# More streamed products in two inverses, an input split behind a mask step, and other PSUM banks for second spans

## The chip, the cores and the metric

The kernel runs on one core of one Trainium2 chip. The metric is the device time of one launch in microseconds. Three launches of the kernel before gave 970.76, 971.34 and 972.85 us; the median is 971.34. Engines are named as in the profile: PE is the matmul engine (TensorE), DVE VectorE, ACT ScalarE, POOL GpSimd, and SP (SyncE) issues most DMAs.

## The reference

One layer of a hybrid decoder on 512 prompt tokens and 8 sequences of 8 new tokens, 576 columns in all. Two branches read the same normalised input: an RWKV-7 branch ("a", 8 heads of 64, a recurrent state per head) and a differential attention ("b"). Their outputs are merged by gates, and a squared-ReLU MLP and a final norm follow.

```python
xn = rmsnorm(x, g_mix)
P = xn @ w_in                                   # 1024 -> RWKV, q/k/v and gate columns
o_a, S = rwkv7_branch(shift_mix(P[:, :1792]), S0)
att = diff_attend(q, k, v, lam)                 # softmax(q1 k1) - lam * softmax(q2 k2)
o_b = rmsnorm(att, subln_g) * (1 - lam_init)
m = gate_a * (o_a @ w_br_a) + gate_b * (o_b @ w_br_b)
x = x + m @ w_out
x = x + square(relu(rmsnorm(x, g_ffn) @ w_up)) @ w_down
y = rmsnorm(x, g_final)
```

In `rwkv7_branch` every step of the state is `S = S * w + (S a) b^T + v k^T`, `y = S r`. The kernel computes it in chunks of 64 tokens.

## The kernel before

**Layout and products.** Channels lie on the 128 partitions, the 576 tokens on the free axis. A float32 product is made from halves: each operand is split into a high half (a copy by ACT in the fp32r type) and a low half (DVE subtracts the high half from the original), and three matmuls are added up in PSUM: high by high, high by low, low by high. The token axis is cut into two spans of 288 columns (`HALF`), so one output block of 128 channels takes 2 spans x the number of 128-row pieces of the contraction x 3 matmuls: 48 for a contraction of 1024, 24 for one of 512. In the profile such a block's weights are `raw_x`, `hi_x`, `lo_x` and its PSUM tile `ps_x`.

**`stream` (L154)** makes such a block as a generator: it loads the weights with SP, splits them, takes one PSUM bank for each span, and yields before each matmul, so that its caller decides between which other instructions the products fall. When a span is finished, an evacuation `evac` reads the bank. `dense` runs a stream to its end at once. `waiting` is a list of streams; `take(n)` puts out the next n products of it, and `fill(n)` does so behind the last matmul issued.

**PSUM.** There are eight banks: two in the pool `psd`, for streams; three in `psw` (`bank`), for short steps; one called `tbank`; and two called `cbank(0)` and `cbank(1)`. The last two hold the scores in attention, and later the steps of the chain.

**The order of the work.** The framework's scheduler sets each engine's instruction order ahead of time by the priority (by default the order in the program), its own estimate of when each instruction could run, and by hand-written constraints: `tc.issue_after(ins)` puts the instructions of a block behind `ins` on the engine of `ins`. On the chip each engine then runs its list in that order.

**The RWKV part.** `rwkv(hp)` (L753) handles a group of two heads, `hp` = 0 to 3, as a generator with stages:

- Stage 1 (to L849) makes decays and keys, and extracts the matrices A of the chunks: matmuls into the banks `pA`, which DVE clips with a mask into `ABR` and `ST` (L843, L847).
- Stage 2 (to L889) makes transposes (`pV`, `pK`) and applies the entering states (`pI`).
- Stage 3 (to L948) inverts the triangular A in four levels. Each level has two visits to PE by `blocks` (L903): 32x32 matmuls into `pW`, copied by ACT into `W`; 32x32 matmuls into `pZ`, which DVE adds to `X` and transposes into `Y`. Behind each visit's small matmuls stand nine streamed products, `take(9)`. Then `pWc` and `pC` follow.
- Stages 4 to 7 finish the samples' states (`pF`), the norm of the output `y` (mean, variance, a power by POOL), and the branch output `oa`, by the transposes `pTy` and the gate product `pg`.

`chain(pr)` (L1016) runs the eight chunks in order for two groups at once, with `cbank` 0 and 1 in turn (`pch`).

The driver (L1106 to L1130) puts the gate columns' streams (`gate`, `ps_g`) on the list, and runs the stages of the four groups with `take` calls between them. The third inverse (hp = 2) and the last one (hp = 3) use up the first five of one half of the gate streams. Then eight streams `branch_b(d)` (`ps_brb`) and the three gate streams left are put on the list, in turn, and `chain(1)` and the last stages follow.

**The second branch.** The attention output lies in DRAM as `ob_d`. `branch_b` calls `ob_halves` (L461) once: four loads into tiles `ob`, four copies by ACT to the high halves and four subtractions by DVE to the low halves (`obh`). Each `branch_b(d)` then loads the gate tile `gb`, streams 24 products, and multiplies the gate tile by each finished span. The tiles `ob` and `gb` share one tag of six buffers.

**After the branches.** At L1143 eight blocks of the first branch's product (`ps_bra`) are evacuated into the merged halves `mh` and `ml`; then come the output projection (`ps_wo`, with a tile `xr` of the input added), the MLP's first layer (`up_pair`, PSUM tiles `ua`, `ub`, `uc`, `ud`, `ux`) and its second (`ps_dn`). The last quarter of the second layer (L1361) runs over the tokens in two unequal spans (320 and 256 columns) with eight streams of one span each; its evacuation writes `fin`.

## Time and profile before

The profile is of one execution.

| | |
|---|---|
| Times of three launches (us) | 970.76, 971.34, 972.85 |
| The profiled execution's own time (us) | 971.81 |
| Its span, first to last instruction (us) | 970.0 |
| Mean granted TensorE clock | 0.996 |
| PE busy | 947.0 us, 10120 matmuls |
| ACT busy | 508.4 us, 1120 instructions |
| DMA | 105.75 MB, mean 109 GB/s |
| The third inverse's visits | from 375.5 us of the span |
| The last inverse's visits | from 402.8 us |
| Chain of the last two groups | 421 to 467 us |
| First branch's product (`ps_bra`) | from 493.8 us |
| MLP's first layer | from 571 us |
| Last quarter of its second layer | 906 to 960 us |

Rows of the profile read like this. A row of a timeline has the start in us from the span's start, the duration in us, engine, line, operation, tiles (out<-in), shapes, the count of merged instructions, and in brackets the idle time of the engine just before, with what ended it. A row of the chain of waits has start, duration and what the end of the kernel depended on. A row of the list of waits has who waited for whom, the total in us, the number of times, and the longest. A line number can be that of a helper: L58 is every ACT copy, L61 every DVE tensor-tensor operation, L72 every matmul. Matmuls are pipelined, and their ends are modelled.

### The profile page before, as it was taken

What the parts mean: (1) busy time and instruction counts of PE and PEld (TensorE: products, weight loads), DVE (VectorE), ACT (ScalarE), POOL (GpSimd) and SP (SyncE); (2) the same over time, 40 slices, a digit from 0 to 9 for tenths busy, and PEclk for the clock granted to TensorE, in tenths of its full rate; (3) what the DMA queues carried; (4) which work ended last, traced back from release to release, by engine and by line L of the source; (5) the groups of instructions that cost most, each with busy time, mean ns of one, the idle gap of its engine ahead of it and who ended that gap; (6) DMA issues with size and microseconds to landing.
All of it is one profiled execution on the core that took longest, in us unless ns stands there. A gap on an engine that the chain in (4) does not pass through costs nothing.

```text
span 970.0 us, 24610 instructions
## 1 busy us (share of the span) xinstructions
PE 947.0 (98%) x10120; PEld 898.3 (93%) x10120; DVE 675.1 (70%) x1435; ACT 508.4 (52%) x1120; POOL 64.6 (7%) x173
## 2 busy tenths in 40 slices
PE   9999999999999998999999999999999999999996
PEld 9999999888987897888999999999999999999996
DVE  6598676776555967455787989866666666666744
ACT  6577465556344564553444767444444444444732
POOL 2601100100000210000100000000000000000001
PEclk9999999999999999999999999999999999999998
DMA  8322663211213234222687532222222222220402
GB/s 271 120 87 91 187 224 117 93 35 47 68 58 102 83 103 168 72 84 74 198 260 236 159 95 98 92 88 88 87 88 88 88 87 88 87 88 23 142 1 97
DMA packets 50833, 105.75 MB, mean 109 GB/s; under 512 B 6066, under 2 KB 8114, under 8 KB 50594
## 3 DMA queue, kind: packets, MB, share of 16 engines
q1 hardware_dynamic: 47442, 96.95, 30.8%
q0 software_dynamic: 1648, 5.35, 1.6%
q10 hardware_dynamic: 1632, 1.89, 0.6%
q8 instruction: 79, 1.29, 0.6%
q14 instruction: 32, 0.26, 0.1%
HBM read 89.38 MB, written 14.78 MB: 107 GB/s over the span
## 4 chain that ended last, share of the span: by engine, by line
PE 56%; DVE 2%; ACT 1%; issue 1%; DMA 1%; POOL 0%; DVEq 0%
PE ps_dn L72 21%; PE ua L1275 5%; PE ux L1275 5%; PE ps_wo L72 4%; PE ps_g L72 4%; PE ps_bra L72 3%; PE uc L1275 3%; PE ub L1275 3%; PE ps_brb L72 3%; PE ud L1275 2%; PE pch L1032 2%; DMA raw_dn<-in_w_down_dram 1%; PE pZ L72 1%; PE pW L72 1%; DVE ya L61 0%
## 5 line engine op out<-in xcount | busy, mean ns | idle before, releaser
L72 PE MATMUL ps_dn<-q,hi_dn 128*128 128x288 f32 x768 | 154.7, 296 | 0.0
L72 PEld LDWEIGHTS ps_dn<-q,hi_dn 128*128 128x128 f32 x768 | 122.8, 188 | 1.4
L72 PE MATMUL ps_dn<-q,lo_dn 128*128 128x288 f32 x384 | 113.2, 295 | 0.0
L72 PE MATMUL ps_g<-xh,lo_g 128*128 128x288 f32 x256 | 78.8, 308 | 0.0
L72 PE MATMUL ps_g<-xl,hi_g 128*128 128x288 f32 x256 | 77.7, 304 | 0.0
L72 PE MATMUL ps_g<-xh,hi_g 128*128 128x288 f32 x256 | 77.4, 302 | 0.0
L72 PEld LDWEIGHTS ps_dn<-q,lo_dn 128*128 128x128 f32 x384 | 72.0, 188 | 0.0
L72 PE MATMUL ps_z<-xh,lo_z 128*128 128x288 f32 (+1 forms) x224 | 69.7, 311 | 0.0
L72 PE MATMUL ps_z<-xl,hi_z 128*128 128x288 f32 (+1 forms) x224 | 67.1, 299 | 0.0
L72 PE MATMUL ps_z<-xh,hi_z 128*128 128x288 f32 (+1 forms) x224 | 66.9, 299 | 0.0
L61 DVE TENSOR_TENSOR ya<-ya,ps_dn 128x288 f32<-128x288 f32 x96 | 43.3, 451 | 27.6 <-PE ps_dn L72 27.5
L58 ACT ACTIVATE hi_dn<-raw_dn 128x512 fp32r<-128x512 f32 x48 | 30.1, 628 | 56.2 <-PE ps_dn L72 56.1
L58 ACT ACTIVATE c<-c 128x288 f32<-128x288 f32 x112 | 48.7, 440 | 9.4 <-DVE c L61 7.7
L1275 PE MATMUL ux<-h_t,hi 128*128 128x288 f32 x256 | 52.4, 296 | 0.0
L1275 PE MATMUL ua<-h_b,hi 128*128 128x288 f32 x256 | 52.2, 296 | 0.0
L58 ACT ACTIVATE hi<-a 128x1024 fp32r<-128x1024 f32 (+1 forms) x32 | 27.1, 846 | 43.2 <-PE ps_dn L72 34.9
L72 PEld LDWEIGHTS ps_g<-xh,lo_g 128*128 128x128 f32 x256 | 48.1, 188 | 1.5 <-issue 0.2
L72 PEld LDWEIGHTS ps_g<-xh,hi_g 128*128 128x128 f32 x256 | 48.2, 188 | 1.3 <-issue 0.2
L72 PEld LDWEIGHTS ps_g<-xl,hi_g 128*128 128x128 f32 x256 | 48.2, 188 | 1.3 <-issue 0.2
L72 PE MATMUL ps_dn<-q,w 128*128 128x320 f32 (+1 forms) x336 | 46.6, 298 | 0.4 <-DVE fin L61 0.4
L61 DVE TENSOR_TENSOR lo<-s,hi 128x1024 fp32r<-128x1024 f32 x32 | 39.2, 1224 | 10.2 <-ACT hi L58 10.0
L72 PEld LDWEIGHTS ps_dn<-q,w 128*128 128x128 f32 x336 | 45.2, 190 | 0.8 <-DVE fin L61 0.7
(390 smaller groups left out, 2721.4 us busy)
## 6 DMA issues: line engine op xcount, KB each, us to landing
a<-in_w_up_dram SPq DMA_DIRECT2D x32, 512.0 KB, 3.3
raw_dn<-in_w_down_dram SPq DMA_DIRECT2D x64, 256.0 KB, 2.7
raw_g<-in_w_in_dram SPq DMA_DIRECT2D x32, 256.0 KB, 3.0
raw_z<-in_w_in_dram SPq DMA_DIRECT2D x28, 256.0 KB, 2.9
gt_d<-gg SPq DMA_DIRECT2D x16, 288.0 KB, 2.4
g<-gt_d SPq DMA_DIRECT2D x16, 288.0 KB, 4.0
kp<-in_ktab_dram SPq DMA_DIRECT2D x16, 256.0 KB, 3.7
vp<-in_vtab_dram SPq DMA_DIRECT2D x16, 256.0 KB, 3.6
```

Source lines behind the costliest of these rows:

```text
L58: ring["act"] = AE.activation(out=out, in_=in_, func=func, **kw)
L61: ins = (eng or VE).tensor_tensor(out=out, in0=a, in1=b, op=op)
L72: ring["mm"] = PE.matmul(out=out, lhsT=lhsT, rhs=rhs, start=start, stop=stop)
L1032: ring["mm"] = PE.matmul(out=ps[rows, e], lhsT=lhs, rhs=rhs, start=first and e == 1, stop=True, skip_group_check=True)
L1275: ring["mm"] = PE.matmul(out=ps[:, :288], lhsT=l[:, k], rhs=hb[blk][:, h, k], start=start and i == 0, stop=i == 11, skip_group_check=skip)
```

## The change

There are three parts.

1. `blocks` puts ten streamed products behind each visit in place of nine when `hp` is 2 or 3.
2. The four high and four low halves of the second branch's input (`ob_halves`) are ordered behind stage 1 of the last group. At its end, stage 1 keeps the last ACT instruction and the last DVE tensor-tensor instruction issued (`own["cut"]`); the latter is the last clip of A, the former the copy of `ST` ahead of the extraction. The high halves go behind the one, the low halves behind the other.
3. `stream` gets an argument `pick`, a list with a `cbank` number or `None` for each span. The second span of `branch_b(d)` for d >= 3 and of every `ps_bra` block goes to `cbank(d % 2)`. In the last quarter of the second MLP layer the streams with odd d go to `cbank(d // 2 % 2)`.

```diff
     def stream(src, kt, xh, xl, spans, evac, name, raws=None, together=False, banks=None,
-               keep=None):
+               keep=None, pick=None):
...
-        pss = banks or [psd.tile([P, 512], F32, tag="d", name=f"ps_{name}_{i}") for i in range(len(spans))]
+        pss = banks or [cbank(pick[i], f"ps_{name}_{i}") if pick and pick[i] is not None else
+                        psd.tile([P, 512], F32, tag="d", name=f"ps_{name}_{i}") for i in range(len(spans))]
...
-            act(hi[h][:, :NT], o_)
-            tt(lo[h][:, :NT], o_, f32(hi[h][:, :NT]), SUB)
+            with tc.issue_after(pair[1]["cut"][0].ins):
+                act(hi[h][:, :NT], o_)
+            with tc.issue_after(pair[1]["cut"][1].ins):
+                tt(lo[h][:, :NT], o_, f32(hi[h][:, :NT]), SUB)
         return hi, lo
 
+    pair = {}
     ob = []
...
-        yield from stream(w_brb[d], HB, ob[0], ob[1], HALF, ev, f"brb_{d}")
+        yield from stream(w_brb[d], HB, ob[0], ob[1], HALF, ev, f"brb_{d}",
+                          pick=(None, d % 2) if d >= 3 else None)
...
-    pair = {}
     halves = [(par, slice(64 * par, 64 * par + 64)) for par in range(2)]
...
                     tt(clip(ST[par], c0, cn)[oth], x[1][oth], m3(c[oth, mk:mk + P], cn), MUL)
+        own["cut"] = ring["act"], ring["tt"]
...
             with tc.issue_after(last.ins):
-                take(9)
+                take(9 if hp < 2 else 10)
...
-        dense(w_bra[d], HB, [o[:, 0] for o in oab], [o[:, 1] for o in oab], HALF, ev, f"bra_{d}")
+        dense(w_bra[d], HB, [o[:, 0] for o in oab], [o[:, 1] for o in oab], HALF, ev, f"bra_{d}",
+              pick=(None, d % 2))
...
-            s_ = stream(None if t0 else w_down[3, d], KT, qh, ql, ((t0, n),), ev, f"dn3{d}_{t0}", keep=rows[d])
+            s_ = stream(None if t0 else w_down[3, d], KT, qh, ql, ((t0, n),), ev, f"dn3{d}_{t0}", keep=rows[d],
+                        pick=(d // 2 % 2,) if d % 2 else None)
```

## The prediction, made before the changed kernel was run

> **What bounds the kernel now.** I read the page's head first, then the list of TensorE's waits.

> ```profile
> span 970.0 us, 24610 instructions
> PE 947.0 (98%) x10120; PEld 898.3 (93%) x10120; DVE 675.1 (70%) x1435; ACT 508.4 (52%) x1120; POOL 64.6 (7%) x173
> PE pA L72 <- DVE ABR L61: 2.6, 4, 1.5
> PE pZ L72 <- issue: 1.8, 2, 1.1
> PE ps_brb L72 <- DVE gb L66: 1.2, 2, 0.7
> ```

> TensorE is busy for 98% of the span, so no engine can be relieved to much effect; only its 23 us of idle time can be won, and the change removes no matmul. The waits (total us, times, longest) name three candidates near the edits; a fourth, ps_dn after fin, is in the timeline below. An idle figure understates a stop, because a product's modelled end lies 0.29 us after its start while the next one could start much sooner. The pace comes from the chain of waits, and the stops from TensorE's timeline:

> ```profile
> 494.00 25.65 PE ps_bra L72 x192
> 914.13 24.26 PE ps_dn L72 x168
> 371.20 0.40 PE L72 MATMUL ps_g<-xl,hi_g 128*128 128x288 f32 x1
> 373.12 1.29 PE L72 MATMUL pA<-ST,KB 64*64 64x128 f32 x32 [1.52 <-DVE ABR L61]
> 477.14 0.50 PE L72 MATMUL ps_brb<-obh,hi_brb 128*128 128x288 f32 x2 [0.69 <-DVE gb L66]
> 477.48 0.29 PE L72 MATMUL ps_brb<-obh,lo_brb 128*128 128x288 f32 x1
> 492.15 0.53 PE L72 MATMUL ps_brb<-obh,hi_brb 128*128 128x288 f32 x2 [0.55 <-DVE gb L66]
> 912.96 0.75 PE L72 MATMUL ps_dn<-q,w 128*128 128x320 f32 x4
> 914.13 0.70 PE L72 MATMUL ps_dn<-q,w 128*128 128x320 f32 x3 [0.42 <-DVE fin L61]
> ```

> 25.65/192 is 0.134 us a product of 288 columns, 24.26/168 is 0.144 for the last stage's. So a stop loses its idle time plus 0.29 - 0.13 = 0.16, and a little for restarting: after the stop at 477.14 two products take 0.50, so the second starts 0.21 after the first, 0.08 late. At 492.15 that is 0.10, at 914.13 about 0.10.

> **Part 1, the input split behind A.** VectorE and ScalarE around the first stop:

> ```profile
> 369.26 0.45 DVE L61 TENSOR_TENSOR gg<-ps_g,R 128x288 f32<-128x288 f32 x1
> 371.70 0.76 DVE L61 TENSOR_TENSOR obh<-ob,obh 128x576 fp32r<-128x576 f32 x1 [1.99 <-ACT obh L58]
> 372.38 0.88 DVE L61 TENSOR_TENSOR ABR<-pA,cst_sb 128x512 f32<-128x512 f32 x2
> 370.98 0.68 ACT L58 ACTIVATE obh<-ob 128x576 fp32r<-128x576 f32 x1 [1.11 <-DMA ob<-ob_d]
> 369.94 1.32 PE L72 MATMUL pA<-ST,KB 64*64 64x128 f32 x40
> 368.68 4.12 SPq L485 DMA_DIRECT2D gb<-gt_d  x4
> 379.12 0.33 SPq L150 DMA_DIRECT2D raw_g<-in_w_in_dram  x1
> 389.39 0.63 ACT L58 ACTIVATE hi_g<-raw_g 128x512 fp32r<-128x512 f32 x1 [1.40 <-PE ps_g L72]
> ```

> VectorE runs in order. From 369.71 it stood before the low half of the split (obh), which waited for ScalarE's high half, which waited for ob's load. The first group of pA was done at 369.94 + 1.32 = 371.26, but its reader, the ABR clip, stood behind and began at 372.38. TensorE needs the clips to free banks, and lost 373.12 - 371.20 - 0.13 = 1.79. With the low halves behind the last clip the first one can start at about 371.3, **1.1 earlier**; the other 0.7 stays, since TensorE resumes 0.74 after the clips begin. Bounds: 0.4, if another piece of some 0.7 takes the place in front, and all of 1.79, if the order fills it with products. I take 1.1, the row nearest.

> What moves: two low halves (the one at 371.70 and one just before gg; the other two are behind the clips already) come behind them, 2 x 0.76 us; on ScalarE one high half of 0.68 is held until the copy of ST ahead of pA, of no weight. In the SyncE queue the four gb loads (the row of 4.12 us) wait for tiles that the split frees; the last of them will stand until the second low half is done, about 378, with raw_g behind it. That weight load leaves at 379.12 anyway and is first read about 389.39, so even a few us of delay cost 0. Nothing moves on GpSimd's queue.

> Where the two low halves land is the second group's inverse, in front of something that TensorE waits for:

> ```profile
> L61 DVE TENSOR_TENSOR X<-X,pZ 128x288 f32<-128x288 f32 (+1 forms) x4 | 1.7, 436 | 3.8 <-PE pZ L72 3.8
> 388.40 0.42 DVE L61 TENSOR_TENSOR X<-X,pZ 128x256 f32<-128x256 f32 x1 [0.89 <-PE pZ L72]
> 388.36 1.38 PE ps_g L72 x9
> 389.74 0.68 PE pW L72 x50
> 382.76 1.13 issue
> 415.03 1.26 PE ps_g L72 x8
> 416.21 0.75 PE L72 MATMUL pW<-X,DM 32*32 32x32 f32 x64
> 416.90 0.65 PE L76 MATMUL pTy<-cst_sb,y 128*128 128x128 f32 x4
> 417.58 0.95 PE L72 MATMUL pZ<-W,Y 32*32 32x32 f32 x64
> 417.59 2.02 ACT L58 ACTIVATE oa<-pTy 64x256 f32<-64x256 f32 x6
> ```

> Between 375.9 and 395.4 VectorE waits 3.8 us for pZ alone, so 1.5 us fits. X of one visit ends at 388.82, and the pW that reads it starts near 389.7: 0.85 spare. One low half (0.76) in front is just covered.

> **Part 2, ten products a visit.** In these two inverses nine products already cover each visit: 9 take 1.38 with the change of shape, and the next burst follows. So the tenth removes no steady wait; it lengthens the cover by 0.13, to about 0.98, which is what the displaced low halves need. I put gain and cost there at 0 (bounds: 1.5 lost, if both low halves fall where nothing is spare; 0.2 gained at the first pZ).

> The tenth is taken from somewhere. The list of streamed products in front of the second branch runs out in the last inverse: counted in the timeline, its eight visits get 9, 9, 9, 9, 9, 8, 0, 0 = 53. The third inverse will take 8 more, leaving 45 = 10, 10, 10, 10, 5, 0, 0, 0. So the sixth visit is bare too and the fifth half bare: 8 products, 1.07 us, of cover are gone there. The visit at 416.21 shows what a bare one does: four pTy transposes fill it and pZ starts at 417.58. More such work is due there, and the second branch's products have their operands. I charge **0.4** (bounds 0 and 1.07).

> **Part 3, banks for second spans.** Now a product stream's two spans take both `psd` banks, and the next stream waits for an evacuation that stands in VectorE's queue behind other work:

> ```profile
> 475.27 0.76 DVE L61 TENSOR_TENSOR y<-y,var 128x576 f32<-128x576 f32 x1 [1.50 <-POOL var L243]
> 476.56 0.44 DVE L66 SCALAR_TENSOR_TENSOR gb<-gb,ps_brb 128x288 f32<-128x288 f32 x1
> 913.59 0.48 DVE L61 TENSOR_TENSOR fin<-ps_dn,ya 128x320 f32<-128x320 f32 x1
> ```

> With second spans in the chain's banks, idle once the chain has ended, a stream needs only one `psd` bank and the next has the other. Both brb stops go: 0.69 + 0.16 + 0.08 + 0.55 + 0.16 + 0.10 = 1.74. In the last projection the third stream no longer needs the bank of the first: 0.42 + 0.16 + 0.10 = **0.68** (0.3 if the queue that held `fin` holds the next bank as well). The bra stream has no stop in its 25.65 us, so its banks are worth 0 by themselves; they matter for what is late next:

> ```profile
> 493.84:519.49 25.65, 25.65 (x194) 25.65 (x193) 22.93 (x54) 10.72 (x23) 0.00 (x0) 1.00 0.80 252
> 493.65 0.45 DVE L61 TENSOR_TENSOR oab<-oa,oab 128x288 fp32r<-128x288 f32 x1
> 520.80 0.69 DVE L61 TENSOR_TENSOR lo_wo<-raw_wo,hi_wo 128x512 fp32r<-128x512 f32 x1
> 521.89 0.90 SPq L1182 DMA_DIRECT2D xr<-in_xT_dram  x2
> 525.78 0.46 DVE L61 TENSOR_TENSOR ya<-ps_wo,xr 128x288 f32<-128x288 f32 x1 [3.92 <-PE ps_wo L72]
> ```

> In the window of bra (stretch, length, then PE, PEld, DVE busy) VectorE works 22.93 of 25.65 us. The last oab half is first read 21 products into bra, 2.8 us after its start: it ends at 494.1 and is wanted at 496.8, so 2.7 us spare for an earlier arrival of at most 1.74. At the other end the load of xr follows lo_wo, and the evacuation at 525.78 follows the load; if VectorE is late there, TensorE stops for it. About 0.9 of the 1.74 pulls VectorE's own work along (the pTy transposes of the last two groups follow in order behind the first stop); the other 0.8 must come out of its 2.7 us of idle time in bra. I take **1.45** of 1.74 (bounds 0.9 and 1.74).

> **The sum.** 1.1 + 1.45 + 0.68 - 0.4 = 2.83 us. The profiled execution took 971.81 (span 970.0, 1.8 around it), so it would take 968.98. It lies 0.47 above the median of the runs shown, 971.34; from that median the forecast is **968.5**.

> **Instruction supply.** The wait of 1.13 "issue" at 382.76 lies inside one burst of little matmuls (pZ), with no engine to blame, and the second of the two, 0.7, lies in the last inverse. [...]

> **Rivals.**
> 1. *Instruction stops move.* Ten products shift every burst against whatever makes the two stops, now 1.8 together. Against: two stops in sixteen visits are few. If there are two more like these, 2.83 - 1.8 = 1.03 gained: 970.3. (None at all would give 966.7.)
> 2. *VectorE or xr takes over behind brb.* Then 0.2 of the 1.74 remains: 1.1 + 0.2 + 0.68 - 0.4 = 1.58: 969.8. For it: 520.80 to 525.78 is already tight. Against: 2.7 us of idle time in bra.
> 3. *The split does not leave the way.* If ScalarE's high halves, held only behind the copy of ST, or other VectorE work still stand before the clips, the 1.1 is missing: 1.73 gained, 969.6. For it: pA of the other groups waits too, (2.6 - 1.5) over three places.
> 4. *The last inverse runs bare (slower).* If nothing fills visits five to eight, each of 3.5 visits idles some 0.7 (1.37 from the pW at 416.21 to its pZ, less 0.68 of burst), 2.45; with the six oa copies (2.02) in front of one W and the two low halves (1.5) in front of X it is 6.0, against 1.1 + 1.45 + 0.68 = 3.23 won: 2.8 slower, 974.1. It decides once TensorE idles over 3.2 us there. Against: pTy, pg and brb products are ready to fill.

> **Chances.** Forecast 0.60, rival 1 0.10, rival 2 0.13, rival 3 0.09, rival 4 0.08. The range leaves out rival 4 and the far ends. A difference of 0.2% (1.94 us) is about what a measurement of this kernel can tell from no change. Rivals 1 to 3 gain less than that: faster 0.60, same 0.32, slower 0.08. The range takes in rivals 1 to 3 and the upper bounds, 4.2 for the three parts and part of the 1.8 of instruction stops: 966.2 to 971.0.

> **What would show it.** Right: pA's longest wait falls from 1.5 to some 0.5; the waits of ps_brb for gb and of ps_dn for fin vanish from TensorE's list; bra still runs at 0.134 a product; the stop of ps_wo for ya stays under 0.5. Wrong: new waits of pZ, pW or pWc for W or X in the last inverse, "issue" well off 1.8, or ps_wo's wait grown by what brb won.

## The result, and the profile after

Fourteen runs of the changed kernel have a median of 969.34 us (968.59 to 970.70), beside 972.54 us (970.76 to 975.04) for fourteen of the kernel before: ratio 0.9964, 95% interval 0.9956 to 0.9972, so 0.36% faster. The profiled execution took 968.82 us with a span of 967.0, against 971.81 and 970.0.

The head of the page after and TensorE's list of waits (who waited for whom: total us, times, longest):

```profile
span 967.0 us, 24611 instructions
PE 944.7 (98%) x10120; PEld 896.4 (93%) x10120; DVE 675.4 (70%) x1435; ACT 509.2 (53%) x1120; POOL 64.1 (7%) x173
PE pZ L72 <- issue: 1.4, 3, 0.7
PE pA L72 <- DVE ABR L61: 1.3, 4, 0.7
PE ps_wo L72 <- DVE ya L61: 0.7, 1, 0.7
PE pI L72 <- ACT SVU L58: 0.7, 1, 0.7
```

Of the waits that the prediction read, ps_brb for gb and ps_dn for fin are gone, pA's total is halved, ps_wo's for ya has grown, and pI's for SVU is new. The place of the split in the timeline after:

```profile
371.31 0.40 PE L72 MATMUL ps_g<-xl,hi_g 128*128 128x288 f32 x1
371.94 1.29 PE L72 MATMUL pA<-ST,KB 64*64 64x128 f32 x32 [0.24 <-DVE ABR L61]
371.20 0.89 DVE L61 TENSOR_TENSOR ABR<-pA,cst_sb 128x512 f32<-128x512 f32 x2 [1.51 <-PE pA L72]
381.37 1.39 DVE L61 TENSOR_TENSOR obh<-ob,obh 128x576 fp32r<-128x576 f32 x2
377.96 0.33 SPq L150 DMA_DIRECT2D raw_g<-in_w_in_dram  x1
```

The clips begin at 371.20, as soon as pA is done, and no longer at 372.38. From the last gate product to the next pA it is now 0.63 us where it was 1.92: 1.29 won. The four profiles without the split (the kernel before and three of the experiments below) show 1.42, 1.66, 1.92 and 2.05 there, so the gain is 0.8 to 1.4, and 1.1 on average. The low halves stand in the third inverse (two of them at 381.37), and raw_g still leaves at 378, held by the gb loads as forecast.

The two stretches of part 3, each from the first product that could gain to the first instruction behind it: start and end, length, then busy time and count of PE, PEld, DVE, ACT and POOL, the granted clock, DMA share and GB/s. The kernel before:

```profile
473.12:493.84 20.72, 19.48 (x141) 18.46 (x139) 15.59 (x34) 9.98 (x24) 3.60 (x2) 1.00 0.69 221
906.51:959.81 53.30, 52.88 (x395) 52.28 (x394) 30.55 (x66) 22.98 (x49) 2.76 (x3) 1.00 0.21 70
```

The changed kernel:

```profile
472.20:491.19 18.99, 18.99 (x141) 18.42 (x140) 14.69 (x32) 10.00 (x24) 3.60 (x2) 1.00 0.65 214
904.25:956.87 52.62, 52.62 (x396) 52.28 (x395) 30.44 (x66) 22.91 (x48) 2.75 (x3) 1.00 0.22 71
```

The same matmuls, 1.73 and 0.68 us shorter, and in both TensorE is now busy from end to end. What part 3 won in the first stretch is partly lost where the output projection starts. Rows of the changed kernel around its first evacuation:

```profile
518.70 0.69 DVE L61 TENSOR_TENSOR lo_wo<-raw_wo,hi_wo 128x512 fp32r<-128x512 f32 x1
519.79 0.90 SPq L1188 DMA_DIRECT2D xr<-in_xT_dram  x2
523.50 0.46 DVE L61 TENSOR_TENSOR ya<-ps_wo,xr 128x288 f32<-128x288 f32 x1 [3.74 <-DMA xr<-in_xT_dram]
524.01 0.40 PE L72 MATMUL ps_wo<-mh,hi_wo 128*128 128x288 f32 x1 [0.69 <-DVE ya L61]
```

And the same stop in the kernel before:

```profile
526.29 0.40 PE L72 MATMUL ps_wo<-mh,hi_wo 128*128 128x288 f32 x1 [0.26 <-DVE ya L61]
```

The load of xr stands in the SyncE queue behind a load of raw_wo, and that one waits until VectorE's subtraction lo_wo has freed a weight buffer. So xr leaves 1.1 us after lo_wo begins, in both kernels; it lands at 523.4, and TensorE stops 0.69 us for the evacuation, where it stopped 0.26 before. In the kernels with bra's new banks lo_wo begins the later, the longer VectorE has waited in bra for the loads of the gate tiles g. The kernel before and four with these banks, three of them from the experiments below (us; lo_wo and xr are counted from the start of ps_wo):

| Kernel | VectorE waits for g in bra | lo_wo begins | xr leaves | ps_wo waits for ya |
|---|---|---|---|---|
| before | 0.60 | 1.31 | 2.40 | 0.26 |
| all but the split | 1.74 | 1.57 | 2.66 | 0.58 |
| changed | 2.10 | 1.92 | 3.01 | 0.69 |
| banks alone | 3.05 | 2.87 | 3.96 | 1.61 |
| all but the ten products | 3.33 | 3.04 | 4.13 | 1.94 |

The rows go together; no run moved the loads of g, and why they land later in some kernels than in others stays open.

How far TensorE is ahead of the kernel before, by the starts of the same matmuls (us from the span's start):

| Start of | before | after | ahead | change |
|---|---|---|---|---|
| third inverse (first pW) | 375.45 | 374.28 | 1.17 | +1.28, split; -0.11 ahead of it |
| the last matmuls of the chain | 466.14 | 465.22 | 0.92 | -0.25, ten products |
| ps_bra | 493.84 | 491.19 | 2.65 | +1.73, brb's banks |
| ps_wo | 519.49 | 516.78 | 2.71 | +0.06 |
| MLP's first layer (uc) | 571.41 | 569.13 | 2.28 | -0.43, ya |
| last quarter of the second layer | 906.51 | 904.25 | 2.26 | -0.02 |
| last sums (pst) | 959.81 | 956.87 | 2.94 | +0.68, dn's banks |
| end of the span | 970.04 | 967.05 | 2.99 | +0.05 |

The -0.11 is what two chances leave. From 11 us on the changed kernel was 0.55 ahead, after a start that differs between the two profiles, and it lost that in the first two inverses, where stops with no engine to blame take 1.7 us in it and 0.5 in the kernel before.

### The profile page after: what moved, and what is told of

It is laid out like the page before. It is cut to its first block, busy times and chain, and to the rows that moved or that the text cites. A ratio compares the mean times of both kernels' runs of the same rounds, so it can differ in the third digit from the quotient of the medians.

```text
span 967.0 us, 24611 instructions
## 1 busy us (share of the span) xinstructions
PE 944.7 (98%) x10120; PEld 896.4 (93%) x10120; DVE 675.4 (70%) x1435; ACT 509.2 (53%) x1120; POOL 64.1 (7%) x173
## 3 DMA queue, kind: packets, MB, share of 16 engines
q8 instruction: 79, 1.29, 0.6%
## 4 chain that ended last, share of the span: by engine, by line
PE 69%; ACT 3%; DVE 2%; issue 1%; DMA 0%; POOL 0%; DVEq 0%; ACTq 0%
PE ps_dn L72 21%; PE ps_g L72 10%; PE ux L1281 5%; PE ua L1281 5%; PE ps_wo L72 4%; PE pch L1037 3%; PE ps_z L72 3%; PE ud L1281 3%; PE ub L1281 3%; PE ps_bra L72 3%; PE ps_brb L72 3%; PE uc L1281 3%; PE pZ L72 1%; PE pW L72 1%; ACT TT L58 0%
## 5 line engine op out<-in xcount | busy, mean ns | idle before, releaser
L72 PE MATMUL ps_dn<-q,hi_dn 128*128 128x288 f32 x768 | 154.7, 296 | 0.0
L72 PEld LDWEIGHTS ps_dn<-q,hi_dn 128*128 128x128 f32 x768 | 122.8, 188 | 1.4
L72 PE MATMUL ps_dn<-q,lo_dn 128*128 128x288 f32 x384 | 113.2, 295 | 0.0
L72 PE MATMUL ps_g<-xh,lo_g 128*128 128x288 f32 x256 | 78.2, 305 | 0.0
L72 PE MATMUL ps_g<-xh,hi_g 128*128 128x288 f32 x256 | 77.9, 304 | 0.0
L72 PE MATMUL ps_g<-xl,hi_g 128*128 128x288 f32 x256 | 77.9, 304 | 0.0
L72 PEld LDWEIGHTS ps_dn<-q,lo_dn 128*128 128x128 f32 x384 | 72.0, 188 | 0.0
L72 PE MATMUL ps_z<-xh,lo_z 128*128 128x288 f32 (+1 forms) x224 | 69.7, 311 | 0.0
L72 PE MATMUL ps_z<-xl,hi_z 128*128 128x288 f32 (+1 forms) x224 | 67.1, 300 | 0.0
L72 PE MATMUL ps_z<-xh,hi_z 128*128 128x288 f32 (+1 forms) x224 | 66.9, 299 | 0.0
L61 DVE TENSOR_TENSOR ya<-ya,ps_dn 128x288 f32<-128x288 f32 x96 | 43.3, 451 | 27.6 <-PE ps_dn L72 27.5
L58 ACT ACTIVATE hi_dn<-raw_dn 128x512 fp32r<-128x512 f32 x48 | 30.1, 627 | 56.2 <-PE ps_dn L72 56.1
L58 ACT ACTIVATE c<-c 128x288 f32<-128x288 f32 x112 | 48.7, 439 | 9.3 <-DVE c L61 7.6
L58 ACT ACTIVATE hi<-a 128x1024 fp32r<-128x1024 f32 (+1 forms) x32 | 27.1, 846 | 43.3 <-PE ps_dn L72 34.9
L72 PEld LDWEIGHTS ps_g<-xl,hi_g 128*128 128x128 f32 x256 | 48.2, 188 | 1.5 <-issue 0.2
L72 PEld LDWEIGHTS ps_g<-xh,hi_g 128*128 128x128 f32 x256 | 48.2, 188 | 1.4 <-issue 0.2
L72 PEld LDWEIGHTS ps_g<-xh,lo_g 128*128 128x128 f32 x256 | 48.2, 188 | 1.3 <-issue 0.2
L72 PE MATMUL ps_dn<-q,w 128*128 128x320 f32 (+1 forms) x336 | 46.3, 297 | 0.0
L61 DVE TENSOR_TENSOR lo<-s,hi 128x1024 fp32r<-128x1024 f32 x32 | 39.2, 1224 | 10.2 <-ACT hi L58 10.0
L72 PEld LDWEIGHTS ps_dn<-q,w 128*128 128x128 f32 x336 | 45.3, 190 | 0.1
```

Of the source, the lines that this page charges most:

```text
L58: ring["act"] = AE.activation(out=out, in_=in_, func=func, **kw)
L61: ins = (eng or VE).tensor_tensor(out=out, in0=a, in1=b, op=op)
L72: ring["mm"] = PE.matmul(out=out, lhsT=lhsT, rhs=rhs, start=start, stop=stop)
```

## The experiments

Each run was timed in five rounds beside the kernel before (972.3 to 973.1 us there); ratios are to that.

**One part, or all but one.** Six runs: the split alone, the banks alone, ten products alone, all but the ten products, all but the split, all but the banks. The edits put the lines of the kernel before back:

```diff
-                take(9 if hp < 2 else 10)
+                take(9)
...
-            with tc.issue_after(pair[1]["cut"][0].ins):
-                act(hi[h][:, :NT], o_)
-            with tc.issue_after(pair[1]["cut"][1].ins):
-                tt(lo[h][:, :NT], o_, f32(hi[h][:, :NT]), SUB)
+            act(hi[h][:, :NT], o_)
+            tt(lo[h][:, :NT], o_, f32(hi[h][:, :NT]), SUB)
...
-        yield from stream(w_brb[d], HB, ob[0], ob[1], HALF, ev, f"brb_{d}",
-                          pick=(None, d % 2) if d >= 3 else None)
+        yield from stream(w_brb[d], HB, ob[0], ob[1], HALF, ev, f"brb_{d}")
```

(and the same for the banks of bra and dn.)

The split alone:

> Only the split behind the last extraction of A; nine products, old banks. If the parts add up: the long wait of pA for ABR falls from 1.5 us to about 0.25, the point where the last pW burst of stage 3 begins comes 1.2 earlier, and 0.9 to 1.3 us of the whole is won (ratio 0.9987 to 0.9991); the waits of ps_brb for gb (1.2 us) and of ps_dn for fin (0.4) stay. If the tenth product is what makes the split pay: the two low halves that now land in the third inverse show as new waits of pZ or pW of 0.5 us or more, and the whole gains 0.5 or less.

The banks alone:

> Only the chain's banks for second spans (brb from d = 3, bra, last projection). If the parts add up: both ps_brb stops go (1.74 us won up to the start of bra), ps_wo's wait for ya grows by about 0.4, ps_dn's wait for fin goes (0.68): 1.7 to 2.4 us won, ratio about 0.998; pA's wait of 1.5 stays. If the banks only help together with the split: under 1 us.

Ten products alone:

> Only ten products a visit in the two inverses. If nine already cover every visit: nothing won in the third inverse, and the last one loses 0 to 1.1 us because its list runs out a visit earlier, so 0 to 1.1 slower up to the end of the chain. If nine leave waits that the profile hides: faster by 0.3 us or more by the end of the third inverse, counted at equal products.

All but the ten products:

> The whole change but with nine products a visit. If the tenth costs by the bare visits of the last inverse: 0 to 0.8 us faster than the changed kernel (ratio against the kernel before 0.9955 to 0.9964), and the waits of pg for oa and of pch for TT in the last inverse shrink. If the tenth covers the displaced low halves: 0.5 us or more slower than the changed kernel, with waits of pZ or pW for W or X in the third inverse.

All but the split:

> The whole change but with the split where it was. If the 1.3 us that the split wins at pA stays won: pA's longest wait 1.0 to 1.7 us again and 0.9 to 1.5 us slower than the changed kernel (ratio against the kernel before 0.9974 to 0.9980). If it is given back in the inverses behind it, as the split alone (0.9998) suggests: 0.9960 to 0.9968. If the wait at pA also brings the half clock in some executions: slower by more than 1.5 us in the median, and a wider spread of times.

All but the banks:

> Split and ten products, no second spans in the chain's banks. Theory: the split wins some 1 us where ten products stand behind it, the tenth some 0.1 to 1, the stops at brb (0.69 and 0.55) and at dn (0.42) stay: 2.1 us above the changed kernel, 971 to 972 beside a kernel before at 972.5, ratio 0.998 to 0.999; brb73 to bra 20.7, dn to pst 53.3 to 53.8. Rival (the parts only count together): no gain without the banks, ratio 0.9995 to 1.0005.

| Kernel | median us | ratio, 95% interval | gate product to pA | brb to bra | dn to pst |
|---|---|---|---|---|---|
| split alone | 972.99 | 0.9998, 0.9989 to 1.0007 | 0.63 | 20.71 | 53.47 |
| banks alone | 970.85 | 0.9977, 0.9966 to 0.9987 | 2.05 | 18.98 | 52.62 |
| ten alone | 972.18 | 0.9986, 0.9976 to 0.9995 | 1.42 | 20.74 | 53.83 |
| all but ten | 969.85 | 0.9965, 0.9954 to 0.9976 | 0.64 | 18.99 | 52.62 |
| all but split | 970.32 | 0.9974, 0.9963 to 0.9985 | 1.66 | 18.98 | 52.62 |
| all but banks | 972.49 | 1.0001, 0.9992 to 1.0010 | 0.64 | 20.73 | 53.99 |

(The last three columns are stretches of each profile in us.) At its own place each part does the same in every kernel that has it: the split brings 0.63, the banks 18.98 and 52.62. In the time only the banks are plain: with them the ratio is lower by 0.0023, 0.0033, 0.0012 and 0.0037 in the four pairs that differ in them alone (the fourth is all three against all but the banks), on average 0.0026, or 2.5 us. The split's four pairs give -0.0002, +0.0015, -0.0012 and -0.0010, the ten products' -0.0014, +0.0003, -0.0003 and -0.0001. With intervals of some 0.001 to each ratio, the averages, -0.0002 and -0.0004, can't be told from nothing. So what was expected of the split alone (0.9987 to 0.9991) and of all but the banks (0.998 to 0.999) was missed: neither is shown to be faster than the kernel before.

**What the tenth product costs.** From the start of the third inverse to the end of the chain every kernel puts out the same matmuls (1958 rows before and after). This stretch lasted 90.69 us before and 90.94 after. Stops with no engine to blame fall into it, of a size that differs from profile to profile; summed over the bursts of the two inverses (starts of neighbouring little matmuls, less 8.7 ns each) they are 2.57 and 1.83 us. Without them it lasts 88.12 before, 88.36 with all but ten, but 88.99 to 89.17 in the nine kernels that have the tenth product and this order (the changed one 89.11): **0.9 us more**. The two other kernels with nine products have a stretch at half clock in it and can't be set beside these. Counted up to the first pW of the last inverse, where ten a visit have put out eight products more (1.07 us), it is 25.87 before, 26.13 with all but ten and 27.40 in the changed kernel: 0.46 or 0.20 lost by there. From there to the end of the chain it is 62.2, 62.2 and 61.7, the last with the eight products fewer: 0.55 lost. Two rows of the changed kernel show a stop of each part:

```profile
398.79 0.88 PE L72 MATMUL pI<-ST,s 64*64 64x16 f32 x24 [0.68 <-ACT SVU L58]
416.76 0.75 PE L72 MATMUL pg<-P,wg 128*128 128x288 f32 x2 [0.36 <-ACT oa L58]
```

In front of the last group's pI TensorE waits 0.68 for the copies of SVU, which the kernel before didn't. No products are missing there: eight stand right in front of pI in both kernels. The order has changed: with ten products a visit three pV transposes stand behind pWc and no longer ahead of it, and ScalarE copies SVU behind the TT copies. Its row before, and after:

```profile
394.13 1.55 ACT L58 ACTIVATE SVU<-pV 64x256 f32<-64x256 f32 x4 [0.33 <-PE pV L76]
```
```profile
396.73 0.77 ACT L58 ACTIVATE SVU<-pV 64x256 f32<-64x256 f32 x2
```

The row of pg is one of the bare visits of the last inverse; that wait for oa is new too, and so is one of 0.5 of the chain (pch) for TT. The stop at pI is larger than the loss up to the last inverse; why the stretch in front of it is shorter by the rest, no run shows.

**The bare visits filled.** A sixth gate stream goes ahead of the second branch, so that all eight visits of the last inverse get ten products:

```diff
-    waiting += ga[:5]
+    waiting += ga[:6]
...
-    waiting += [x for d in range(KT) for x in [branch_b(d)] + ga[5:][d:d + 1]]
+    waiting += [x for d in range(KT) for x in [branch_b(d)] + ga[6:][d:d + 1]]
```

> The changed kernel with one more gate stream on the list ahead of the last inverse, so that no visit runs bare. If bare visits cost what I charged: the waits of pg for oa, of pZ for W and of pch for TT in the last inverse go, up to 1.1 us won by the start of the chain; at the end of the chain there are fewer products left to cover the norm, so pTy may wait for y up to 2 us. Sum between 0.8 faster and 1 slower than the changed kernel. If the bare visits cost nothing: the start of the chain at equal products does not move.

972.55 us, ratio 0.9999 (0.9989 to 1.0008): it gives back all that the change won, where 1 us slower was the most expected. The row behind it, in the timeline of this kernel:

```profile
496.53 1.19 PE L72 MATMUL ps_bra<-oab,hi_bra 128*128 128x288 f32 x5 [2.03 <-ACT oab L58]
```

With the visits full, the pTy and pg steps that stood in them come behind; bra starts 1.3 us later, oab is late, and TensorE stops 2.03 us in bra, 28.4 us from ps_bra to ps_wo instead of 25.6. So the bare visits are no hole: they hold the work that bra needs.

**Bra's banks taken away.**

```diff
-        dense(w_bra[d], HB, [o[:, 0] for o in oab], [o[:, 1] for o in oab], HALF, ev, f"bra_{d}",
-              pick=(None, d % 2))
+        dense(w_bra[d], HB, [o[:, 0] for o in oab], [o[:, 1] for o in oab], HALF, ev, f"bra_{d}")
```

> The changed kernel without the banks for the bra stream. If VectorE's idle time there is enough: bra still runs 25.5 to 25.7 us for its 192 products and the time is that of the changed kernel within 0.3 us. If VectorE is late after an earlier start: stops of ps_bra for g, 0.5 us or more, and wo starts that much later.

970.13 us, ratio 0.9972 (0.9959 to 0.9985). The window of bra in this kernel (columns as above), and its wait:

```profile
491.39:517.75 26.36, 26.06 (x194) 25.65 (x193) 23.52 (x56) 10.84 (x23) 0.00 (x0) 1.00 0.80 266
```
```profile
PE ps_bra L72 <- DVE g L66: 0.2, 1, 0.2
```

Bra takes 26.36 instead of 25.59, and TensorE waits there for g, which VectorE writes; in the kernel before, with the same two banks but the brb stops in front of it, it took 25.65. But from ps_wo to uc it then takes 51.76 instead of 52.35, so that uc starts 569.51 instead of 569.13, and 0.21 of this it had lost by the end of the chain already. 0.77 lost in one stretch leave about 0.2 after the next: VectorE's work sets the pace there (the wait for ya is 0.13 in this kernel), and a stop removed from bra comes back as the wait for ya. In the time the two kernels can't be told apart.

**xr's load first.** The first xr goes ahead of the later raw_wo loads on the SyncE queue:

```diff
-    hfs = {}
+    hfs, xrs = {}, []
...
-            nc.sync.dma_start(out=xr, in_=xT[:, d])
+            xrs.append(nc.sync.dma_start(out=xr, in_=xT[:, d]))
...
-        dense(w_out[d], KT, mh, ml, HALF[::1 if d < 4 else -1], ev, f"wo{d}")
+        with tc.issue_after(xrs[0].ins) if i else nullcontext():
+            dense(w_out[d], KT, mh, ml, HALF[::1 if d < 4 else -1], ev, f"wo{d}")
```

> The changed kernel with the output projection's second and later weight loads ordered behind the first load of xr on SyncE. If the late xr takes back part of what the banks win: ps_wo's wait for ya (0.7 us in the changed kernel, 1.6 and 1.9 in two others with these banks) falls under 0.2, no half clock behind it, 0.4 to 1.5 us faster than the changed kernel (ratio against the kernel before 0.995 to 0.996). If another wait ends last there (lo_wo or the region's release): the same time, with the wait under a new name.

968.68 us, ratio 0.9958 (0.9944 to 0.9971); the interval covers the changed kernel's 0.9964. Rows of it:

```profile
514.21 0.86 SPq L1188 DMA_DIRECT2D xr<-in_xT_dram  x2
526.33 0.40 PE L72 MATMUL ps_wo<-mh,hi_wo 128*128 128x288 f32 x1 [0.28 <-DVE ya L61]
527.30 0.40 PE L72 MATMUL ps_wo<-mh,lo_wo 128*128 128x288 f32 x1 [0.44 <-DVE lo_wo L61]
```

xr leaves 5.6 us earlier in the span, lands at 519.6, and the wait for ya is 0.28 instead of 0.69, but a wait of 0.44 for lo_wo stands behind it, and the stretch from ps_wo to uc falls from 52.35 to 52.24 only. The load was late, but it was late by VectorE's work, and with the load early that work itself is what TensorE waits for.

**The stops with no engine to blame.** In nearly all profiles they come at the same number in TensorE's list of matmuls, whatever work stands there: 4792 in all ten of the kernels so far (0.49 to 1.60 us), 5557 in nine (0.05 to 1.84), others at 2246, 3137, 4919, 5684 and 5812, a whole number of steps of some 127.4 apart. The next kernel has 21 matmuls more in the warm-up at the start, which leave 42 records (two for each float32 matmul), and no other difference in order:

```diff
-        for _ in range(9):
-            mm(up[:, :P], onesP, onesP)
+        for w in [P] * 9 + [1] * 21:
+            mm(up[:, :w], onesP, onesP[:, :w])
```

> The changed kernel with 21 matmuls of one column more in the warm-up at the start (42 records of PE's list, since a float32 matmul leaves two), where PE waits 1.53 us for ScalarE anyway; every other instruction of every engine stays in its order. In the runs so far the stops inside bursts of 32x32 matmuls come at the same record numbers of PE's list in all kernels (4792 in ten of ten, 5557 in nine of ten, smaller ones at 2246, 3137, 4919, 5684, 5812), about 127.4 records apart, and they are the larger the later in its burst the record lies: under 0.15 us up to the 20th, 0.3 at the 40th, 0.5 to 1.6 from the 53rd on. Theory A (instructions arrive in blocks of a fixed number, and the next block shows as a stop where a burst has used up what was queued): the bursts move by 42, the record numbers don't; so no stop at 4792 (now the 15th of its burst) and 5557 (13th), new ones of 0.4 to 1.5 us at 4665 (51st), 4920 (60th), 5430 (49th), 5685 (58th) and 3264 (56th). Sum of the stops within bursts of all four inverses 3 to 6 us (3.5 in the changed kernel's profile); time 969.3 to 972, 0 to +2 us against the changed kernel. Rival B (the stops belong to the work, to DMAs or to a moment of the run): the same matmuls stop as before, at records 4834 and 5599, and the time is that of the changed kernel within 0.5 us.

Rows of the kernel before, of the changed one, and of this one:

```profile
382.04 0.72 PE L72 MATMUL pZ<-W,Y 32*32 32x32 f32 x60
383.89 0.31 PE L72 MATMUL pZ<-W,Y 32*32 32x32 f32 x12 [1.13 <-issue]
```
```profile
381.17 0.69 PE L72 MATMUL pZ<-W,Y 32*32 32x32 f32 x57
382.44 0.32 PE L72 MATMUL pZ<-W,Y 32*32 32x32 f32 x15 [0.59 <-issue]
```
```profile
387.17 0.64 PE L72 MATMUL pZ<-W,Y 32*32 32x32 f32 x51
388.39 0.38 PE L72 MATMUL pZ<-W,Y 32*32 32x32 f32 x21 [0.58 <-issue]
394.76 0.72 PE L72 MATMUL pW<-X,DM 32*32 32x32 f32 x61
396.24 0.25 PE L72 MATMUL pW<-X,DM 32*32 32x32 f32 x3 [0.76 <-issue]
```

The count in front of the break is the place in the burst: 60 with nine products, 57 with ten, and with 42 records more the stops are in other bursts. By record numbers:

| Record | place in its burst: before, after, shifted | stop in us: before, after, shifted |
|---|---|---|
| 4664 | 13, 11, 51 | none, none, 0.78 |
| 4792 | 60, 57, 15 | 1.31, 0.77, none |
| 4920 | 34, 29, 61 | none, none, 0.95 |
| 5557 | 66, 55, 13 | 0.84, 0.26, none |
| 5685 | 40, 32, 59 | none, 0.26 (at 5684), 1.01 |

So the stops belong to the number in TensorE's list of matmuls, as the first theory forecast, and not to the work. What makes them, no run shows. Of the new ones named only 5430, the 49th of its burst, is missing, and 3265 has 1.08. The time, 978.41 us (ratio 1.0064, 1.0044 to 1.0084), is far above what was expected of it, and the reason is the added matmuls themselves:

```profile
1.12 12.87 PEld L72 LDWEIGHTS warmup<-onesP 128*128 128x128 f32 x60 [1.12 <-DVE s L1409]
```

60 weight loads take 12.87 us, 0.21 each, as much with one column behind them as with 128 (18 of the latter take 3.91 in the kernel before). That is at half rate: up to 17.2 us the products of this kernel start 0.24 us apart, and 0.13 later. The first product starts at 13.94 instead of 6.49, and 7.5 of the 9.1 us are gone by then.

**Six records more.** The same with three matmuls on the kernel with xr first, once with one column, once with 32x32 weights (`[32] * 3`, `onesP[:w, :w]`). The first:

> The kernel with xr's load first (x1_xr_first) and 3 matmuls of one column more in the warm-up (6 records), every other order unchanged. Theory A: the two large stops fall on the 51st and 49th record of their bursts instead of the 57th and 55th, 2246 on the 47th; each loses some 0.3 us, and no other boundary comes into the end of a burst: 0.5 to 1.2 us less in the bursts (sum 4.2 there before), time 967.5 to 968.5. Rival B: 968.7 within 0.5 as x1_xr_first, the same matmuls stopping.

The second:

> As f6_xr_shift (xr's load first, 6 records more in the warm-up), but the three matmuls have 32x32 weights and 32 columns in place of 128x128 weights and one column, since those took the time of full ones at the start. Theory A: stops at the same records as in f6_xr_shift, 4792 and 5557 each under 0.6 us, the sum within the bursts of all four inverses 0.8 to 2.2 us (1.2 in f6_xr_shift, 4.2 in x1_xr_first); the three matmuls cost under 0.2 us ahead of a wait of over 0.6 for hi_q; time 967.0 to 968.5, ratio 0.994 to 0.996, the fastest of all. Rival: the stops come back elsewhere, or the low sum was that one execution's, and the time stays at x1_xr_first's 968.7 or the 969.5 of f6_xr_shift: ratio 0.996 to 0.997.

The stops shrank as expected: summed over the four inverses 1.16 and 1.07 us, where xr first alone had 4.24, the changed kernel 3.49, and no other profile under 2.27. At 4792 they are 0.24 and 0.21, at 5557 0.47 and 0.21. The times did not follow: 969.46 (ratio 0.9964, 0.9952 to 0.9977) and 969.23 us (0.9964, 0.9951 to 0.9977). In the profile of the second, the stretch from the third inverse to the end of the chain is 2.44 us shorter than with xr first (89.70 for 92.14), but the output projection up to uc 0.86 longer (53.10 for 52.24), with a new wait of ps_wo for ml, and 1.1 us are lost in the first 11 us, around a stretch at half clock. Whether the added records bring the latter on, two profiles can't say. No kernel here is shown to be faster than the changed one.

## Why the prediction was right, step by step

- **Split: 1.1 forecast, 1.29 at its place, 1.1 on the average of the kernels without it.** pA's wait there fell to 0.24, its longest anywhere to 0.7 (some 0.5 forecast). The second group's inverse absorbed the low halves, and raw_g's delay cost nothing. But the time confirms no more than the sum: on the average of four pairs the split is worth 0.2 us, give or take 0.7, and what takes the rest back I can't name.
- **Ten products: -0.4 forecast, -0.25 measured, of two halves that weren't forecast so.** The steady cost is 0.9, close to the upper bound of 1.07. Some 0.55 of it falls from the last inverse on, where the prediction charged the 0.4; the rest, 0.2 to 0.5, falls ahead of it, where the prediction put 0: it overlooked that SVU would come late for pI. The other half, 0.74 of stops less (2.57 to 1.83), is luck of the execution at least in part: on average the stops are 3.08 in the four profiles with nine products and 2.34 in six with ten at the same record numbers, where the two large ones come 3 and 11 matmuls earlier in their bursts. So the two halves about cancel, and all but ten measures the same (0.9965) as all (0.9964).
- **The lists of visits were right**: 10, 10, 10, 10, 5, and then pTy and pg in the bare ones. Rival 4, the slower one, fails for the reason given: the bare visits have work, and filling them with products instead gives back the whole gain.
- **brb's banks: 1.74 at the place forecast, 1.73 measured; 1.45 after rival 2's share, 1.30 measured.** Rival 2 was a cost and not the outcome: ps_wo's wait for ya grew by 0.43. The path was the one that the prediction names (lo_wo, then the load of xr, then the evacuation), but two of its steps failed. VectorE was to make up 0.8 us from its 2.7 us of idle time in bra; it idled 2.95 there all the same, 2.10 of it waiting for g, which the prediction didn't look at. And the wait that "stays under 0.5" is 0.69, and 1.6 and 1.9 in the two kernels with the banks and nine products. With waits of that size the 1.45 would not have held. Bra's own banks, put at 0 by themselves, are worth 0.2 at uc.
- **dn's banks: 0.68 forecast, 0.68 measured**, in each of the kernels of the table that have them.
- **The sum: 2.83 forecast, 2.99 in the profile.** 968.5 came from three runs with a median of 971.34; fourteen have 972.54, and beside them the change wins 3.2 us. That the sum fits so well is in part luck: 0.74 of the 2.99 are the smaller stops, and in the times of the experiments the banks bring 2.5 us (2.13 forecast), the split 0.2 (1.1) and the ten products 0.4 (-0.4), each give or take 0.7, so that errors cancel.
- **The stops with no engine to blame (Instruction supply in the prediction).** The rival, two stops more, did not happen here, but one as large is within what the profiles show at the same record numbers (2.27 to 5.48 over the four inverses). The runs show where they come: a whole number of steps of some 127.4 matmul records apart, whatever work stands there. Where such a number falls behind more than some 50 little matmuls of a burst, the stop is anything from nothing to 1.84 us, both at 5557. What the first theory of the shifted kernel takes for their cause was my guess; no run shows more than the place.

## What to carry to other kernels

Price a stop by its own place, then follow the gain to the next wait that the same engines feed: here 1.73 became 1.30 within 35 us, because the next evacuation's load was queued behind a weight load that VectorE's late work held up. Idle time of an engine is no reserve until its waits are read: VectorE's in bra was a wait for loads. When fillers are moved into one stage, ask which stage they leave, and what the scheduler reorders: the cost of the tenth product came from both. A part of 1 us out of 970 can be exact in every profile and still not show in the time; only the profile's stretches then tell what it did.

## What was not expected of the hardware

**Half a clock after a half-empty stretch.** In several profiles TensorE runs at half clock for one stretch of 3.41 us. Two stretches of the kernel with all but ten, about ps_wo's wait of 1.9 us (clock and DMA share are the third and second numbers from the end):

```profile
523.90:527.31 3.41, 1.48 (x12) 1.24 (x11) 1.03 (x3) 0.54 (x2) 0.00 (x0) 1.00 1.00 330
527.31:530.73 3.42, 3.42 (x17) 3.42 (x16) 2.54 (x7) 2.39 (x6) 0.00 (x0) 0.50 0.90 295
```

And of the kernel with the split alone, about a stop with no engine to blame:

```profile
411.60:415.01 3.41, 1.82 (x43) 1.61 (x47) 1.28 (x3) 0.45 (x1) 0.00 (x0) 1.00 0.02 5
415.01:418.43 3.42, 3.42 (x93) 3.08 (x83) 0.69 (x1) 1.01 (x2) 0.00 (x0) 0.50 0.00 0
```

Idling isn't the only thing ahead of it. In five of the fourteen profiles a stretch near 353 us (361.95 in the shifted kernel) runs at half clock after one in which TensorE was busy throughout by the records. With xr first this is the one from 353.30 (3.41 busy of 3.41 us ahead of it, a clock of 0.50 in it); from ps_g's start at 268 to the split this kernel lost 1.6 us against the changed one. The work there is the same in all: 32 matmuls pI of 16 columns and ten pn of 2 columns, between products of 288 columns. In these five one stretch, counted as above, holds all 2.18 us of the little matmuls; in the other nine an edge cuts them, no stretch holds more than 2.06, and no half clock follows. What decides it, no run was made to show.

Neither the profile of before nor that of after has a stretch at half clock between the two changes of its clock given above.

**A one-column matmul is not a small one.** Each of its two weight loads cost 0.21 us in the warm-up, at the half rate of the start, the same as with 128 columns behind it. That the weights set the time is my reading: among the loads of the warm-up with 32x32 weights the shortest took 0.10 us, in the changed kernel, where all are 128x128, 0.19.
